# A decoder block on one core: the ConvFFN up projection as wide and narrow matmuls, and a gap between an adaLN row's copy and its transposes

## The chip, the cores and the metric

The kernel runs on one core of a Trainium2 chip, as one program in one launch. The metric is the device time in microseconds (us). Before the change the median of three runs is 1520.65 us (1518.46 to 1521.5). The engines named below are PE (TensorE, with PEld for its weight loads), DVE (VectorE), ACT (ScalarE), POOL (GpSimd) and SP (SyncE, whose queue issues nearly all the DMAs).

## The reference

One decoder block on 256 tokens of 2048 channels, all in float32. Two sub-layers, each wrapped in norms and in a shift, a scale and a gate that come from a conditioning vector c (adaLN):

```python
mod = (silu(c) @ w_ada + b_ada)                  # 6 rows of 2048: sh1, sc1, gt1, sh2, sc2, gt2
h = rms_norm(x, g_pre_mix) * (1 + sc1) + sh1
z = h @ w_in                                     # 2048 x 8000
mix = (g_a * mla(z) + g_b * swa(z)) @ w_o        # two attention mixers, gated
x = x + gt1 * rms_norm(mix, g_post_mix)
h = rms_norm(x, g_pre_ffn) * (1 + sc2) + sh2
u = causal_dwconv(h @ w_up, conv_w, conv_b)      # 2048 x 11264, then 3 taps along the tokens
y = (silu(u[:5632]) * u[5632:]) @ w_down         # 5632 x 2048
out = x + gt2 * rms_norm(y, g_post_ffn)
```

## The kernel before

**Precision.** Every large product is made of three float32r matmuls: a float32 operand is split into a high part (a cast on ACT, line 116 for weights and 151 for activations) and a low part (the difference, a subtraction on DVE, lines 117 and 152), and the product is hi*hi + hi*lo + lo*hi, accumulated in one PSUM bank. Lines 129 to 131 (`mm3`) do this with 128x128 weights held in the array and 256 token columns of activations streaming; lines 137 to 139 (`mm3t`) hold the activations and stream 512 columns of weights. The weights come as raw tiles of 512 KB (line 95), each split once and used once. Weight tiles rotate through pools: in the up projection 4 raw, 6 hi and 6 lo tiles.

**Stages.** Norm and first adaLN rows; the input projection; the attention stage; the output projection `down(w_o)`; the sandwich norm, which is a chain of small DVE and ACT steps (lines 672 to 688), then 32 transposes of the result back to channel-major on PE (line 143 for all transposes) and the modulated, split activations `h2` (lines 696, 697, 151, 152); the up projection, 44 steps j of two output blocks q (88 blocks); the down projection `down(w_down)`; the last norm and the stores.

**The up projection.** One block is 16 chunks of 128 input channels times three matmuls, all into the left half of a 512-column PSUM bank: 48 matmuls of 256 columns. A block's weights are two raw tiles; below, such a half block is called a *part* (24 matmuls). When a block is done, ACT makes `u` from the bank with the middle tap and the bias (line 738), and DVE adds the two other taps, reading the bank again (lines 739 and 740). Every second step ends in a SiLU on ACT (743), a product on POOL (746) and a split of the result. The first step's two blocks have their weights loaded during `down(w_o)`; the second step's weights are held back until a late point of the making of `h2`.

**The adaLN rows in the background.** `ada_gen` loads a row block of `w_ada` (512 KB), lets DVE multiply it by c and add it to an accumulator `acc` (lines 233 and 235), and yields; it does so 16 times, then sums `acc` over the partitions with 4 small matmuls (240) and copies the row to SBUF on ACT (242). `cols_gen` runs it for both halves of one row (32 yields) and then turns the row into columns with 4 small matmuls (290) and adds the bias (292). Three such rows (gt1, sc2, sh2, in this order in one list) run during the attention stage and `down(w_o)`, one (gt2) during the up projection. `pump` advances the list: it is called after each raw weight tile and takes a step as soon as `rate` has added up to 1 (rates 0.5, 0.8, 0.3 and 0.5 in four stages). `drain()` after `down(w_o)` runs whatever is left of the three rows.

**Order.** The Python code gives the program order; a list scheduler then places each engine's instructions, so neighbours in the code may be shifted. Each engine and each DMA queue works through its own list strictly as built.

## Time and profile before

| | |
|---|---|
| median of three runs | 1520.65 us |
| the profiled execution, its own time | 1520.17 us |
| its span in the trace | 1518.3 us |
| PE busy | 1472.3 us, 97% |
| PE weight loads busy | 1361.0 us, 90% |
| DVE busy | 1050.1 us, 69% |
| ACT busy | 754.4 us, 50% |
| POOL busy | 286.9 us, 19% |
| mean DMA rate | 235 GB/s |

Busy time is the union of an engine's instructions in the trace. A matmul is shown with a modelled end, so that neighbours overlap: what a stream of matmuls costs is read from the distance of their starts and not from their durations. The stages by time: input projection to about 300 us, attention to 650, `down(w_o)` to 745, the sandwich norm to 756, up projection from 756 to 1269, down projection to the end.

### The profile page before, as it was taken

Reading aid. Unit: us, or ns where it says so; the run is one execution under the profiler, and the core shown is the slowest. Engines: PE = TensorE matmul, PEld = TensorE weight load, DVE = VectorE, ACT = ScalarE, POOL = GpSimd, SP = SyncE. Lnnn points to the kernel's source line nnn. Section 1 sums busy time; section 2 is a strip of 40 time slices with the busy share of each in tenths; the row PEclk is TensorE's granted clock in tenths of the full one; section 3 lists DMA queues with packets and bytes.
Section 4 is the critical chain, followed back from the end, with each engine's and each line's share of the span. In section 5 each row is a group of like instructions: output and inputs, shape, how many; then the busy total and the mean of one; then the engine's idle time right before and its main releaser. Section 6 shows DMA issues by size and latency. Waiting matters only on the chain.

```text
span 1518.3 us, 27322 instructions
## 1 busy us (share of the span) xinstructions
PE 1472.3 (97%) x10914; PEld 1361.0 (90%) x10914; DVE 1050.1 (69%) x1384; ACT 754.4 (50%) x1165; POOL 286.9 (19%) x207
## 2 busy tenths in 40 slices
PE   7999999799999999999899999999999999999998
PEld 6988899789898898978799999999999999888886
DVE  3578868888787969777787777765666665444443
ACT  4534435545654655765564444554554454444342
POOL 0034215832525444320000010000000000000000
PEclk9999999999999999999999999999999999999999
DMA  9889868589587968669477788755556557666662
GB/s 371 295 313 328 308 234 262 178 264 306 175 306 240 298 197 274 197 208 358 183 250 259 254 277 266 225 181 183 182 181 190 182 181 242 191 193 192 194 193 99
DMA packets 101535, 357.14 MB, mean 235 GB/s; under 512 B 11760, under 2 KB 12208, under 8 KB 100896
## 3 DMA queue, kind: packets, MB, share of 16 engines
q1 hardware_dynamic: 99936, 350.82, 69.4%
q0 software_dynamic: 1472, 4.58, 1.2%
q8 instruction: 85, 1.39, 0.4%
q14 instruction: 42, 0.34, 0.1%
HBM read 351.11 MB, written 4.24 MB: 234 GB/s over the span
## 4 chain that ended last, share of the span: by engine, by line
PE 79%; DVE 9%; DMA 7%; issue 3%; ACT 1%; POOL 0%; DVEq 0%; SPq 0%; ACTq 0%; POOLq 0%
PE bk_mm L129 12%; PE bk_mm L131 12%; PE bk_mm L130 12%; PE bk_mm L137 4%; PE bk_mm L138 4%; PE bk_mm L139 4%; DMA raw<-in_w_ada_dram 4%; PE bk_sc L130 4%; PE bk_sc L129 4%; PE bk_sc L131 4%; PE bk_sc L138 3%; PE bk_sc L137 3%; PE bk_sc L139 3%; DVE wlo L117 3%; DVE acc L235 3%
## 5 line engine op out<-in xcount | busy, mean ns | idle before, releaser
L117 DVE TENSOR_TENSOR wlo<-raw,whi 128x1024 fp32r<-128x1024 f32 (+3 forms) x472 | 589.7, 1256 | 317.2 <-ACT whi L116 316.0
L116 ACT CAST whi<-raw 128x1024 fp32r<-128x1024 f32 (+3 forms) x472 | 478.1, 1019 | 531.7 <-PE bk_mm L130 161.6
L129 PE MATMUL bk_mm<-h_hi,whi 128*128 128x256 f32 x1824 | 522.6, 287 | 0.8 <-ACT h_hi L151 0.5
L131 PE MATMUL bk_mm<-h_hi,wlo 128*128 128x256 f32 x1824 | 518.0, 284 | 0.5 <-DVE wlo L117 0.5
L130 PE MATMUL bk_mm<-h_lo,whi 128*128 128x256 f32 x1824 | 518.4, 284 | 0.1
L129 PEld LDWEIGHTS bk_mm<-h_hi,whi 128*128 128x128 f32 x1824 | 350.9, 192 | 14.2 <-issue 8.7
L130 PEld LDWEIGHTS bk_mm<-h_lo,whi 128*128 128x128 f32 x1824 | 351.2, 193 | 1.1 <-issue 0.8
L131 PEld LDWEIGHTS bk_mm<-h_hi,wlo 128*128 128x128 f32 x1824 | 351.2, 193 | 1.2 <-DVE wlo L117 0.7
L235 DVE SCALAR_TENSOR_TENSOR acc<-raw,csil,acc 128x1024 f32<-128x1024 f32 (+1 forms) x141 | 188.6, 1337 | 58.2 <-DMA raw<-in_w_ada_dram 58.0
L129 PE MATMUL bk_sc<-h_hi,whi 128*128 128x256 f32 x560 | 158.7, 283 | 0.0
L130 PE MATMUL bk_sc<-h_lo,whi 128*128 128x256 f32 x560 | 158.6, 283 | 0.0
L131 PE MATMUL bk_sc<-h_hi,wlo 128*128 128x256 f32 x560 | 158.5, 283 | 0.0
L746 POOL TENSOR_TENSOR sa<-sa,u 128x512 f32<-128x512 f32 x22 | 32.7, 1486 | 469.1 <-DVE u L740 447.6
L129 PEld LDWEIGHTS bk_sc<-h_hi,whi 128*128 128x128 f32 x560 | 107.5, 192 | 0.4 <-ACT whi L116 0.4
L130 PEld LDWEIGHTS bk_sc<-h_lo,whi 128*128 128x128 f32 x560 | 107.5, 192 | 0.2 <-DVE h_lo L152 0.2
L131 PEld LDWEIGHTS bk_sc<-h_hi,wlo 128*128 128x128 f32 x560 | 107.5, 192 | 0.0
L363 POOL TENSOR_TENSOR pair<-pair,part 128x512 f32<-128x512 f32 x35 | 64.0, 1830 | 195.2 <-ACT part L362 195.1
L137 PE MATMUL bk_sc<-whi,g_hi 128*128 128x512 f32 x176 | 68.6, 390 | 0.0
L137 PE MATMUL bk_mm<-whi,g_hi 128*128 128x512 f32 x176 | 68.6, 390 | 0.0
L138 PE MATMUL bk_mm<-wlo,g_hi 128*128 128x512 f32 x176 | 68.5, 389 | 0.0
L139 PE MATMUL bk_mm<-whi,g_lo 128*128 128x512 f32 x176 | 68.5, 389 | 0.0
L138 PE MATMUL bk_sc<-wlo,g_hi 128*128 128x512 f32 x176 | 68.5, 389 | 0.0
(202 smaller groups left out, 2102.8 us busy)
## 6 DMA issues: line engine op xcount, KB each, us to landing
raw<-in_w_ada_dram SPq DMA_DIRECT2D x192, 512.0 KB, 5.0
raw<-in_w_up_dram SPq DMA_DIRECT2D x176, 512.0 KB, 4.3
raw<-in_w_in_dram SPq DMA_DIRECT2D x116, 512.0 KB, 5.1
raw<-in_w_down_dram SPq DMA_DIRECT2D x88, 512.0 KB, 4.4
raw<-in_w_o_dram SPq DMA_DIRECT2D x32, 512.0 KB, 5.0
raw<-in_w_uqn_dram SPq DMA_DIRECT2D x16, 384.0 KB, 4.1
bias<-trow POOLq DMA_DIRECT2D x16, 256.0 KB, 5.2
raw<-in_w_ukv_dram SPq DMA_DIRECT2D x16, 256.0 KB, 3.5
```

The source lines that it names most:

```text
L116: act.copy(hi[:, :n], raw[:, :n])
L117: dve.tensor_tensor(lo[:, :n], raw[:, :n], hi[:, :n].bitcast(F32), op=ALU.subtract)
L129: pe.matmul(o, wh, xh, start=start, stop=False)
L130: pe.matmul(o, wh, xl, start=False, stop=False)
L131: pe.matmul(o, wl, xh, start=False, stop=stop)
L137: pe.matmul(o, ch, wh, start=start, stop=False)
L138: pe.matmul(o, ch, wl, start=False, stop=False)
L139: pe.matmul(o, cl, wh, start=False, stop=stop)
L235: dve.scalar_tensor_tensor(acc[:, :w], r, csil[:, j:j + 1], acc[:, :w], op0=ALU.mult, op1=ALU.add)
L363: pool.tensor_tensor(pairs[i][:, :wd], pairs[i][:, :wd], part[:, :wd], op=ALU.add)
L746: pool.tensor_tensor(sa, sa, us[1], op=ALU.mult)
```

## The change

Three things.

1. In the up projection, `mm3w` takes two chunks at once. The activations' high and low part of a chunk now lie side by side in one tile, so one matmul of 512 columns computes hi*hi into the left half of the bank and hi*lo into the right half; then a matmul of 256 columns adds lo*hi to the left half. Two chunks go as wide, wide, narrow, narrow. At a block's end ACT copies the right half to a new SBUF tile `o`, DVE adds the left half to it, and the conv taps (ACT and DVE) read `o` instead of the bank.
2. For that, `split_pair` makes one tile of 1024 columns for two chunks instead of a hi and a lo tile, the pool `hp` has 8 such tiles instead of 16 of half the size, and the last stage's residual tiles are halves of these. The latent tiles of the attention stage keep the old form, written out in place.
3. In `cols_gen`, four bare yields stand between the second half's copy and the transposing matmuls. Each takes one step of `pump` without doing anything.

```diff
@@ -49,7 +49,7 @@
     const = ctx.enter_context(tc.tile_pool(name="const", bufs=1))
     dram = ctx.enter_context(tc.tile_pool(name="dram", bufs=1, space=bass.MemoryType.DRAM))
     hp_ctx = ExitStack()
-    hp = hp_ctx.enter_context(tc.tile_pool(name="hp", bufs=16, side="right"))
+    hp = hp_ctx.enter_context(tc.tile_pool(name="hp", bufs=8, side="right"))
     w_ctx = ExitStack()
     W = {"pool": w_ctx.enter_context(tc.tile_pool(name="wp1", bufs=1)), "n": NW1}
     psp = ctx.enter_context(tc.tile_pool(name="psp", bufs=1, space=PS))
@@ -125,14 +125,21 @@
 
     def mm3(o, w, x, start, stop):
 
-        (wh, wl), (xh, xl) = w, x
+        (wh, wl), (xh, xl, _) = w, x
         pe.matmul(o, wh, xh, start=start, stop=False)
         pe.matmul(o, wh, xl, start=False, stop=False)
         pe.matmul(o, wl, xh, start=False, stop=stop)
 
+    def mm3w(o, ws, xs, start, stop):
+
+        for i, (w, x) in enumerate(zip(ws, xs)):
+            pe.matmul(o, w[0], x[2], start=start and i == 0, stop=False)
+        for i, (w, x) in enumerate(zip(ws, xs)):
+            pe.matmul(o[:, :T], w[1], x[0], start=False, stop=stop and i == 1)
+
     def mm3t(o, w, x, half, start, stop):
 
-        (wh, wl), (xh, xl) = w, x
+        (wh, wl), (xh, xl, _) = w, x
         ch, cl = xh[:, half * P:half * P + P], xl[:, half * P:half * P + P]
         pe.matmul(o, ch, wh, start=start, stop=False)
         pe.matmul(o, ch, wl, start=False, stop=False)
@@ -146,12 +153,12 @@
 
     def split_pair(src, pl, tag, bufs, eng=dve):
 
-        hi = pl.tile([P, 512], F32R, tag=tag, bufs=bufs, name=tag + "_hi")
-        lo = pl.tile([P, 512], F32R, tag=tag, bufs=bufs, name=tag + "_lo")
-        i0 = act.copy(hi, src)
-        i1 = eng.tensor_tensor(lo, src, hi.bitcast(F32), op=ALU.subtract)
+        hl = pl.tile([P, 2, 2, T], F32R, tag=tag, bufs=bufs // 2, name=tag)
+        src = src.rearrange("p (j t) -> p j t", j=2)
+        i0 = act.copy(hl[:, :, 0], src)
+        i1 = eng.tensor_tensor(hl[:, :, 1], src, hl[:, :, 0].bitcast(F32), op=ALU.subtract)
         split_ins[:] = [i0, i1]
-        return [(hi[:, j * T:j * T + T], lo[:, j * T:j * T + T]) for j in range(2)]
+        return [(hl[:, j, 0], hl[:, j, 1], hl[:, j].rearrange("p a t -> p (a t)")) for j in range(2)]
 
 
     blk_ctx = ExitStack()
@@ -285,6 +292,9 @@
 
         for half in range(2):
             yield from ada_gen(a["w_ada2"][which][half], T, rows, half * T, None)
+
+        for _ in range(4):
+            yield
         ps = bank("tp")
         for b in range(4):
             pe.matmul(ps[:, 4 * b:4 * b + 4], rows[:, b * P:(b + 1) * P], ident[:, 0:P:32], start=True, stop=True)
@@ -404,7 +414,11 @@
             for j in range(2):
                 v = pr[:, j * T:j * T + T]
                 dve.scalar_tensor_tensor(v, v, gcol[:, gofs + 2 * i + j:gofs + 2 * i + j + 1], r, op0=ALU.mult, op1=ALU.mult)
-            res += split_pair(pr, blkp, "blk", NBLK, pool)
+            hi = blkp.tile([P, 512], F32R, tag="blk", name="blk_hi")
+            lo = blkp.tile([P, 512], F32R, tag="blk", name="blk_lo")
+            act.copy(hi, pr)
+            pool.tensor_tensor(lo, pr, hi.bitcast(F32), op=ALU.subtract)
+            res += [(hi[:, j * T:j * T + T], lo[:, j * T:j * T + T], None) for j in range(2)]
 
     def rope(x, n):
 
@@ -714,26 +728,28 @@
         e = j % 2
         if e == 0:
             us = [up.tile([P, 512], F32, tag=f"u{q}", name="u") for q in range(2)]
-        bs = [bank2()[:, :T] for q in range(2)]
+        bs = [bank2() for q in range(2)]
         if j == 0:
             wts = up0
-            for k in range(KC):
+            for k in range(0, KC, 2):
                 for q in range(2):
-                    mm3(bs[q], wts[q].cut(k * P), h2[k], k == 0, k == KC - 1)
+                    mm3w(bs[q], [wts[q].cut(i * P) for i in (k, k + 1)], h2[k:k + 2], k == 0, k == KC - 2)
             w_ctx.close()
             W.update(W2)
             ff = ctx.enter_context(tc.tile_pool(name="ff", bufs=1, reuse_waits="tile"))
         for q in range(2):
             fblk = q * NF + j
-            o = bs[q]
             if j:
                 with ExitStack() as order:
                     if j == 1:
                         order.enter_context(tc.issue_after(after_dve.ins))
                         order.enter_context(tc.issue_after(after_act.ins))
                     wt = Weights(a["w_up"][fblk], 2048)
-                for k in range(KC):
-                    mm3(o, wt.cut(k * P), h2[k], k == 0, k == KC - 1)
+                for k in range(0, KC, 2):
+                    mm3w(bs[q], [wt.cut(i * P) for i in (k, k + 1)], h2[k:k + 2], k == 0, k == KC - 2)
+            o = up.tile([P, T], F32, tag="o", name="o")
+            act.copy(o, bs[q][:, T:])
+            dve.tensor_tensor(o, o, bs[q][:, :T], op=ALU.add)
             u = us[q][:, e * T:e * T + T]
             act.activation(u, o, AF.Identity, scale=cw[:, 2, fblk:fblk + 1], bias=cw[:, 3, fblk:fblk + 1])
             dve.scalar_tensor_tensor(u[:, 1:], o[:, :T - 1], cw[:, 1, fblk:fblk + 1], u[:, 1:], op0=ALU.mult, op1=ALU.add)
@@ -749,8 +765,10 @@
     up_ctx.close()
 
     fin = ctx.enter_context(tc.tile_pool(name="fin", bufs=1, reuse_waits="tile"))
-    x2 = [[hp.tile([P, 512], F32, tag="h", name="x2") for g in range(4)] for t in range(2)]
-    y2 = [[hp.tile([P, 512], F32, tag="h", name="y2") for g in range(4)] for t in range(2)]
+    def halves(name):
+        b = [hp.tile([P, 1024], F32, tag="h", name=name) for _ in range(4)]
+        return [[b[2 * t + g // 2][:, g % 2 * 512:g % 2 * 512 + 512] for g in range(4)] for t in range(2)]
+    x2, y2 = halves("x2"), halves("y2")
     for t in range(2):
         for g in range(4):
             nc.sync.dma_start(x2[t][g], x1d[t * P:(t + 1) * P, g * 512:g * 512 + 512])
```

How the instructions move, at three places. The list that PE works through in the up projection, around the end of the gt2 row (`bk_tp<-acc,ones` is the sum over partitions, `bk_tp<-c_ident,rows` the transposing matmuls; `whi`, `wlo` are the weights' parts). Before:

```order
L129 MATMUL bk_sc<-h_hi,whi 128x256
L130 MATMUL bk_sc<-h_lo,whi 128x256
L131 MATMUL bk_sc<-h_hi,wlo 128x256
L240 MATMUL bk_tp<-acc,ones 32x256 x4
L290 MATMUL bk_tp<-c_ident,rows 128x4 x2
L129 MATMUL bk_mm<-h_hi,whi 128x256
...
L129 MATMUL bk_mm<-h_hi,whi 128x256
L130 MATMUL bk_mm<-h_lo,whi 128x256
L290 MATMUL bk_tp<-c_ident,rows 128x4 x2
L131 MATMUL bk_mm<-h_hi,wlo 128x256
```

After, at the same place:

```order
L136 MATMUL bk_sc<-h,whi 128x512 x2
L138 MATMUL bk_sc<-h,wlo 128x256 x2
L247 MATMUL bk_tp<-acc,ones 32x256 x4
L136 MATMUL bk_mm<-h,whi 128x512 x2
...
L136 MATMUL bk_mm<-h,whi 128x512 x2
L138 MATMUL bk_mm<-h,wlo 128x256 x2
L300 MATMUL bk_tp<-c_ident,rows 128x4 x4
L136 MATMUL bk_sc<-h,whi 128x512 x2
```

Two chunks now take four matmuls, two of 512 and two of 256 columns, where six of 256 stood. The four transposing matmuls, of which two stood right behind the sums and two 28 rows later, now stand together 65 rows behind the sums.

The list of the SP queue from the last loads of `down(w_o)` to the stores of the residual (`w_ada_1` is the sh2 row, `w_ada_3` the gt2 row, which the scheduler starts early; `w_up` the first up-projection weights). Before:

```order
L95 DMA raw<-in_w_ada_1_dram 128x1024 x2
L95 DMA raw<-in_w_up_dram 128x1024 x2
L95 DMA raw<-in_w_ada_3_dram 128x1024
L95 DMA raw<-in_w_up_dram 128x1024 x2
L95 DMA raw<-in_w_ada_1_dram 128x1024
L95 DMA raw<-in_w_up_dram 128x1024
L95 DMA raw<-in_w_ada_1_dram 128x1024 x3
L702 DMA x1d<-x_7860 128x2048 x2
L95 DMA raw<-in_w_up_dram 128x1024
```
After:

```order
L95 DMA raw<-in_w_ada_1_dram 128x1024 x2
L95 DMA raw<-in_w_ada_3_dram 128x1024
L95 DMA raw<-in_w_up_dram 128x1024 x4
L95 DMA raw<-in_w_ada_1_dram 128x1024
L95 DMA raw<-in_w_up_dram 128x1024
L95 DMA raw<-in_w_ada_1_dram 128x1024 x9
L716 DMA x1d<-x_7813 128x2048
L95 DMA raw<-in_w_ada_1_dram 128x1024 x2
L716 DMA x1d<-x_7813 128x2048
L95 DMA raw<-in_w_up_dram 128x1024
```

Behind the fourth of the last five `w_up` tiles there stand 4 more loads of the sh2 row before and 12 after, two of them behind the first store. The sh2 row's work has moved towards the end of `down(w_o)`, since the three rows take 12 more steps of `pump`.

The list of DVE from the sandwich norm of the second 128 tokens to the first chunk of `h2` (`acc` is a step of an adaLN row, `ss2s`, `r` the norm, `x` and `yg` the residual and the normed rows, `sh` the finished sh2 columns, `ht` the modulated activations). Before:

```order
L672 TENSOR_REDUCE ss_8578<-ssq 128x1
L654 TENSOR_TENSOR yg<-bk_mm,gate 128x512
L658 RECIPROCAL r_8581<-r_8581 128x1
L658 RECIPROCAL r_8577<-r_8577 128x1
L688 TENSOR_SCALAR yg<-x_7860,r_8581 128x512 x2
L678 SCALAR_TENSOR_TENSOR x_7860<-yg,r_8577,x_7860 128x512 x2
L292 TENSOR_TENSOR sh_148<-bk_tp,c_b_adaT 128x16
L678 SCALAR_TENSOR_TENSOR x_7860<-yg,r_8577,x_7860 128x512 x2
L681 TENSOR_REDUCE ss2s<-ss_8580 128x1
L658 RECIPROCAL r_8581<-r_8581 128x1
L688 TENSOR_SCALAR yg<-x_7860,r_8581 128x512 x2
L697 TENSOR_SCALAR ht<-bk_mm,s_147,sh_148 128x256 x2
```
After:

```order
L692 SCALAR_TENSOR_TENSOR x_7813<-yg,r_8561,x_7813 128x512 x4
L672 RECIPROCAL r_8565<-r_8565 128x1
L242 SCALAR_TENSOR_TENSOR acc<-raw,csil,acc 128x1024
L702 TENSOR_SCALAR yg<-x_7813,r_8565 128x512 x2
L695 TENSOR_REDUCE ss2s<-ss_8564 128x1
L242 SCALAR_TENSOR_TENSOR acc<-raw,csil,acc 128x1024
L672 RECIPROCAL r_8565<-r_8565 128x1
L242 SCALAR_TENSOR_TENSOR acc<-raw,csil,acc 128x1024
L702 TENSOR_SCALAR yg<-x_7813,r_8565 128x512 x2
L242 SCALAR_TENSOR_TENSOR acc<-raw,csil,acc 128x1024
L302 TENSOR_TENSOR sh_148<-bk_tp,c_b_adaT 128x16
L711 TENSOR_SCALAR ht<-bk_mm,s_147,sh_148 128x256 x2
```

Before, no step of `acc` is left here and `sh` is ready between two updates of `x`. After, four steps of `acc` stand among the last twelve rows, five more above them back to the first half's norm (where two stood), and `sh` comes last, directly ahead of `ht`.

## Rows read from the trace of the kernel before

**Rows 1.** The page: busy time of the engines, and the chain of waits that ended last, by engine.

```profile
PE 1472.3 (97%) x10914; PEld 1361.0 (90%) x10914; DVE 1050.1 (69%) x1384; ACT 754.4 (50%) x1165; POOL 286.9 (19%) x207
PE 79%; DVE 9%; DMA 7%; issue 3%; ACT 1%; POOL 0%; DVEq 0%; SPq 0%; ACTq 0%; POOLq 0%
```

**Rows 2.** Busy time by stretch: the up projection while the gt2 row runs beside it, and after that. Columns: stretch, its length, busy us (instructions) of PE, PEld, DVE, ACT, POOL, granted clock, DMA share, GB/s.

```profile
752.00:962.00 210.00, 207.33 (x1716) 205.35 (x1717) 164.74 (x196) 109.91 (x143) 15.17 (x9) 0.99 0.77 255
962.00:1264.00 302.00, 302.00 (x2519) 302.00 (x2518) 190.41 (x226) 148.28 (x183) 16.83 (x13) 1.00 0.59 186
```

**Rows 3.** Timeline of PE (start us, duration us), first and last of stretches of back-to-back matmuls: 48 matmuls of 256 columns in the up projection, then 15 matmuls of 512 columns in the down projection.

```profile
1050.54 0.28 PE L129 MATMUL bk_sc<-h_hi,whi 128*128 128x256 f32 x1
...
1056.30 0.28 PE L129 MATMUL bk_mm<-h_hi,whi 128*128 128x256 f32 x1
...
1272.17 0.39 PE L137 MATMUL bk_sc<-whi,g_hi 128*128 128x512 f32 x1
...
1275.57 0.39 PE L137 MATMUL bk_mm<-whi,g_hi 128*128 128x512 f32 x1
```

**Rows 4.** Timeline of DVE through the sandwich norm; in brackets the idle time before a row and what ended it.

```profile
737.94 0.16 DVE L672 TENSOR_REDUCE ss<-ssq 128x1 f32<-128x4 f32 x1 [2.82 <-ACT sqd L651]
...
738.61 1.27 DVE L235 SCALAR_TENSOR_TENSOR acc<-raw,csil,acc 128x1024 f32<-128x1024 f32 x1
...
739.92 1.28 DVE L235 SCALAR_TENSOR_TENSOR acc<-raw,csil,acc 128x1024 f32<-128x1024 f32 x1
741.12 2.73 DVE L678 SCALAR_TENSOR_TENSOR x<-yg,r,x 128x512 f32<-128x512 f32 x4
744.93 0.16 DVE L681 TENSOR_REDUCE ss2s<-ss 128x1 f32<-128x4 f32 x1 [1.07 <-ACT sq L680]
746.04 0.16 DVE L672 TENSOR_REDUCE ss<-ssq 128x1 f32<-128x4 f32 x1 [0.95 <-ACT sqd L651]
...
749.02 0.16 DVE L292 TENSOR_TENSOR sh<-bk_tp,c_b_adaT 128x16 f32<-128x16 f32 x1
...
752.27 0.88 DVE L688 TENSOR_SCALAR yg<-x,r 128x512 f32<-128x512 f32 x2
```

**Rows 5.** Timelines of PE, then ACT, in the same place: the sum, the transposing matmuls of the sh2 row, the transposes of the normed rows, the first up-projection matmul; the row's copy and the first modulated chunk on ACT.

```profile
745.21 0.64 PE L240 MATMUL bk_tp<-acc,ones 128*32 128x256 f32 x8
745.78 1.33 PE L290 MATMUL bk_tp<-c_ident,rows 128*128 128x4 f32 x8
...
752.81 3.68 PE L143 MATMUL bk_mm<-c_ident,yg 128*128 128x128 f32 x17 [4.81 <-DVE yg L688]
756.25 0.36 PE L129 MATMUL bk_sc<-h_hi,whi 128*128 128x256 f32 x1
...
746.09 0.36 ACT L242 COPY rows<-bk_tp 128x256 f32<-128x256 f32 x1
753.75 1.20 ACT L696 ACTIVATE ht<-bk_mm,sh,s 128x256 f32<-128x256 f32 x2
```

**Rows 6.** Who waited for whom (us in total, times, longest) from 780 to 960 us, then from 960 to 1260 us.

```profile
ACT whi L116 <- DMA raw<-in_w_up_dram: 48.5, 31, 3.7
DVE acc L235 <- DMA raw<-in_w_ada_dram: 29.6, 22, 2.8
ACT whi L116 <- PE bk_sc L130: 5.0, 3, 2.9
...
ACT whi L116 <- PE bk_mm L130: 83.4, 61, 2.4
ACT whi L116 <- PE bk_sc L130: 57.0, 42, 1.8
PE bk_tp L290 <- ACT rows L242: 1.9, 1, 1.9
```

**Rows 7.** Timelines of DVE and PE: the low parts of the weights of parts 17 and 66 (50 subtractions, the first and the last shown), and the starts of blocks 5 and 33 on PE (28 blocks apart, so parts 10 and 66).

```profile
798.32 1.22 DVE L117 TENSOR_TENSOR wlo<-raw,whi 128x1024 fp32r<-128x1024 f32 x1
...
944.81 1.21 DVE L117 TENSOR_TENSOR wlo<-raw,whi 128x1024 fp32r<-128x1024 f32 x1
...
786.83 0.28 PE L129 MATMUL bk_sc<-h_hi,whi 128*128 128x256 f32 x1
...
948.86 0.28 PE L129 MATMUL bk_sc<-h_hi,whi 128*128 128x256 f32 x1
```

**Rows 8.** Single lines (durations in ns: least, median, most): the copy of a 256-column PSUM row on ACT, and a two-operand step of DVE with a bank as an operand.

```profile
L242 ACT COPY rows<-bk_tp x8: 359/372/374, 331.2 to 960.5; 128x256 f32<-128x256 f32 x8
L739 DVE SCALAR_TENSOR_TENSOR u<-bk_mm,cw,u x53: 470/476/479, 781.7 to 1271.9; 128x255 f32<-128x255 f32 x53
```

**Rows 9.** Busy time by stretch, columns as in rows 2: three stretches of the attention stage, one while the sandwich norm begins, and two around the restart of PE after it.

```profile
500.00:550.00 50.00, 47.39 (x368) 44.09 (x367) 39.77 (x88) 34.16 (x90) 25.57 (x19) 1.00 0.81 266
550.00:600.00 50.00, 47.89 (x385) 45.47 (x384) 42.90 (x65) 26.07 (x56) 19.04 (x14) 1.00 0.74 245
600.00:650.00 50.00, 48.62 (x337) 43.40 (x337) 37.53 (x92) 33.98 (x82) 18.45 (x17) 0.97 0.61 193
...
735.00:740.00 5.00, 5.00 (x24) 4.14 (x23) 2.18 (x6) 0.98 (x3) 0.00 (x0) 1.00 0.01 4
...
753.00:756.00 3.00, 3.00 (x15) 2.64 (x14) 1.66 (x4) 2.76 (x5) 0.00 (x0) 0.52 0.28 112
756.00:759.00 3.00, 3.00 (x27) 2.76 (x25) 2.80 (x6) 2.54 (x6) 0.00 (x0) 1.00 0.00 0
```

## The prediction

> **What bounds the kernel now.** I read the page first: PE is busy for 97% of the span and makes up 79% of the chain that ended last, DVE 9% and DMA 7% [rows 1]. So time is won where PE's own work shrinks and nothing else is late behind it, and lost wherever PE is made to wait. Then the stretches of the up projection, the stage that the change rewrites: PE is busy 207.3 of 210 us while the gt2 row runs beside it, and all of 302 us after that, at full granted clock, with DVE at 78% and 63% [rows 2]. Next I wanted what a matmul costs, and took it from the distance of starts: 48 matmuls of 256 columns take 5.76 us, 120.0 ns each; 15 of 512 columns take 3.40 us, 226.7 ns each [rows 3]. The 256 columns between the two sizes cost 106.7 ns, so a matmul is 106.7 ns per 256 columns and 13.3 ns on top, whatever its width. Last, the waits: during the first stretch the casts of weights on ACT wait mostly for their loads (48.5 us in 31 waits), in the second for PE to free a tile (83.4 and 57.0 us) [rows 6]. The reader should see two regimes: with the adaLN loads the supply of weights is what runs short, without them PE is.
>
> **The wide matmuls.** The columns stay as they were: two chunks are 6 x 256 before and 2 x 512 + 2 x 256 after. What goes is two of six matmuls, so 16 of a block's 48, and with each of them 13.3 ns [rows 3]. A block falls from 5.76 to 5.55 us, by 0.213; all 88 blocks by 18.7 us.
>
> The Trainium skill speaks against this. TensorE: Matmul & The Clock Gate, section Back-to-back issue gap, gives a warm matmul as its columns over 2.4 GHz plus about 2.5 ns; by that rule the 1408 matmuls fewer are worth 3.5 us, an estimate from that page, and the change as a whole would cost time. The trace does not agree: its two pitches leave 13.3 ns at both widths [rows 3].
>
> **What of it arrives.** PE can gain only while weights are ahead of it. The low parts of parts 17 and 66 begin 146.49 us apart, 2.990 us per part; PE moves at 162.03 / 56 = 2.893 us per part [rows 7]. Part 17 was ready at 799.5 and, seven parts of 2.88 behind 786.83, used at 807.0: a lead of 7.5 us. Part 66 was ready at 946.0 and used at 948.9: 2.8 us. So already before, supply is slower than PE here, and PE lives on its lead. After, PE asks for a part every 2.77 us; the lead is gone after 7.5 / 0.22 = 34 parts, and from there PE runs at the pace of supply. With that pace unchanged, part 66 can come forward by its lead of 2.8 us and no more, instead of the 7.0 of 33 blocks.
>
> Will the pace hold? Each block gets a copy of 256 columns on ACT, as the row copy's 0.37 us, and an addition on DVE, nearest the tap's 0.48 us [rows 8]. Taps and bias then read `o` from SBUF, which I count as equal. In the stretch of 210 us ACT is busy 110 and DVE 165 [rows 2], and both wait for loads there, so their 33 x 0.37 = 12 and 33 x 0.48 = 16 us find room. But both queues work in order: ACT's bias step now waits for DVE's addition, which stands behind steps of `acc` that wait for their loads (29.6 us in 22 waits [rows 6]), and behind ACT's step stand the next casts. The bounds are wide: if all of 0.85 us per block went into the pace it would be 0.43 per part; if the casts' waits for PE (5.0 us in 3 waits [rows 6]) went because PE is quicker, the pace would gain 0.1. I take 0.04, a tenth of the upper bound, since loads end most of the waits: 50 x 0.04 = 2.0 us, which leaves 2.8 - 2.0 = **0.8 us** of the gain in this stretch. From part 66 on PE sets the pace [rows 2, 6], and the two additions are hidden (DVE 190 of 302 us busy): 55 blocks x 0.213 = **11.7 us**.
>
> **The four yields, where they help.** PE stood 1.9 us before the transposing matmuls of gt2, waiting for the row's copy, which was queued on ACT [rows 6]. With the transposes 65 rows later the copy is long done: **1.9 us** won. It is one wait in the whole span; the other three rows have none on PE to lose.
>
> **The four yields, where they cost.** Three rows now need 36 steps each instead of 32, so when `drain()` comes 12 steps are left over, and some 8 loads with their steps of `acc` move from the attention stage to the end of `down(w_o)`. In the new order nine steps of `acc` stand on DVE between the first norm and `ht`, where two stood. Before, the second half's norm begins at 746.04 and sh2 is ready at 749.0, well before `ht` at 753.75 [rows 4, 5]. After, I add DVE's list up from that same 746.04 (PE's end of `down(w_o)` sets it, and the one extra `acc` before it fits the idle 1.07 and 0.95 us there [rows 4]). A step of `acc` takes 1.20 from start to start, the four updates of x 2.7, each pair of yg 0.8, the gate product 0.6, the small steps together 0.6: six `acc` make 7.2, and all of it 12.6, so the last `acc` ends near 758.7. Then come the sum, the copy, the transposing matmuls and the bias, 1.9 us from the first sum to the last transpose in the old order [rows 5], with hops 2.6: `ht` starts near 761.3 instead of 753.75, **7.6 us** later, and PE has nothing else to do. Eight loads of 512 KB in a row need a free DMA: its share is 0.01 at 735 to 740 [rows 9], so I count no wait for them; if the six late steps each waited 1.35 us, as steps of `acc` did on average [rows 6], it would be 15.7. The lower end is 4, if the row's tail overlaps the norm. PE's clock falls to half in this pause now and is full again at 756 [rows 9]; the transposes run ahead of the first matmuls then as now, and at worst 3 us at half clock cost 1.5.
>
> **At nothing.** The joint hi and lo tiles hold the same bytes and are freed by the same stages; the last stage's halves wait for the stage before, long over when they are read. In the attention stage eight steps of `acc` are missing and some instructions change places. PE idles 6.1 of 150 us there [rows 9]: at best all of that goes; at worst as much again is added. I take 0.
>
> **Sum.** Against the profiled execution: 1520.17 - 0.8 - 11.7 - 1.9 + 7.6 = 1513.4 us. The median of the runs is 0.5 above that execution, so **1514 us**.
>
> **Rivals.**
> *The supply keeps up.* If the copy and the addition vanish in waits and casts no longer wait for PE, all 18.7 us arrive: 1520.65 - 18.7 - 1.9 + 7.6 = 1507.7 us. For it: the load waits of rows 6 are idle time. Against it: 2.99 us per part is slower than PE already. 18%.
> *The supply breaks: slower.* ACT's bias step waiting for DVE's addition, itself behind `acc`, holds the next cast, so each tile's load is issued later. The price is 64 parts times the pace lost. The gains of 2.8, 11.7 and 1.9 less the 7.6 leave 8.8 us, so it decides from 0.14 us per part on; at 0.22, half the upper bound, it is 14.1 us: 1525.9 us. For it: the loads already end most casts' waits; against it: ACT is only half busy. 10%.
> *The sh2 row is later still.* At the end of 15.7 us the sum is 8.1 us more: 1522. For it: five raw tiles serve twelve loads in a row; against it: a DMA with nothing else to do. 12%, most of it within 0.2%.
> *A matmul's 13.3 ns is not saved.* If the constant sits with something that the change leaves, as the page's smaller figure would have it, PE gains 3.5 us at the most, on both stretches: 1520.65 - 3.5 - 1.9 + 7.6 = 1522.9. Against it: both pitches. 5%.
>
> **Numbers.** The forecast has 55%. A measurement of this kernel can tell about 0.2% from no change, so faster means under 1517.6 and slower over 1523.7. The forecast's own range is 1508 to 1519, by the bounds of the pace, the pause and the attention stage. Faster: nearly all of the forecast and the first rival, with a small part of the late row, 0.74. Same: the rest of the forecast, most of the late row and of the unsaved constant, 0.16. Slower: 0.10. The range of 8 in 10 takes in half of the first rival and the edge of the late row: 1505 to 1520.
>
> **What would show it.** In the trace after: wide matmuls 226.7 ns and narrow ones 120 ns apart, in a block of 5.55 us from 970 us on (else the 13.3 ns is wrong); gaps on PE in the second half of the gt2 stretch, behind `whi` or `wlo` (no gaps: the first rival; gaps from its beginning: the second); a pause on PE between `down(w_o)` and the first up-projection matmul near 18.6 us instead of 11, ended by sh2; no wait at the transposing matmuls of gt2. The forecast is wrong if that pause stays as it was, or if the gt2 stretch is longer than 210 us plus the pause.

## The result, and the profile after

The changed kernel takes **1529.24 us** (median of 8 runs, 1522.83 to 1531.02), the kernel before, beside it on the same chip, 1520.16 (8 runs): ratio **1.0056**, 95% interval 1.0041 to 1.0070. Forecast were 1514 us and a range of 1505 to 1520. The change costs 9 us where 6 were to be won, and the time lies outside the range.

The profiled execution took 1522.83 us (span 1521.1), the fastest of the eight; a second profile of the same instructions in the same order, below, took 1527.41 (span 1525.6). Three marks on the timelines of PE and ACT divide the loss:

| us | before | after | after, again |
|---|---|---|---|
| last matmul of `down(w_o)` starts | 744.9 | 754.7 | 755.3 |
| first `ht` starts (ACT) | 753.8 | 771.0 | 772.3 |
| last up-projection matmul starts | 1269.3 | 1271.7 | 1276.3 |
| first `ht` to last up matmul | 515.5 | 500.7 | 504.0 |

So 10 us are lost before `down(w_o)` ends, 7.4 to 8.1 more before `ht`, and the up projection gives 14.8 back in the one execution, 11.5 in the other. The last two were forecast; the first 10 us were not.

**The pause.** PE's waits from 735 to 800 us, then DVE's rows from the second half's sum to the last late step of `acc` and to the finished sh2 columns:

```profile
PE bk_mm L150 <- DVE yg L702: 8.4, 1, 8.4
PE bk_mm L150 <- ACT yg L700: 1.6, 1, 1.6
PE bk_mm L150 <- DVE ht L711: 1.5, 1, 1.5
```

```profile
755.87 0.16 DVE L686 TENSOR_REDUCE ss<-ssq 128x1 f32<-128x4 f32 x1 [0.98 <-ACT sqd L665]
...
767.13 1.28 DVE L242 SCALAR_TENSOR_TENSOR acc<-raw,csil,acc 128x1024 f32<-128x1024 f32 x1
770.76 0.18 DVE L302 TENSOR_TENSOR sh<-bk_tp,c_b_adaT 128x16 f32<-128x16 f32 x1 [2.36 <-PE bk_tp L300]
```

These answer to [rows 4, 5]. From the second half's sum to the end of the last late `acc` DVE needs 767.13 + 1.28 - 755.87 = 12.5 us; sh2 is ready 2.4 us later, and `ht` starts at 771.0.

**The up projection.** One block of 32 matmuls on PE's timeline, from the first wide pair of one block to that of the next (a row holds two back-to-back matmuls):

```profile
1054.49 0.63 PE L136 MATMUL bk_mm<-h,whi 128*128 128x512 f32 x2
1054.96 0.39 PE L138 MATMUL bk_mm<-h,wlo 128*128 128x256 f32 x2
1055.19 0.62 PE L136 MATMUL bk_mm<-h,whi 128*128 128x512 f32 x2
...
1060.06 0.63 PE L136 MATMUL bk_sc<-h,whi 128*128 128x512 f32 x2
```

A block takes 1060.06 - 1054.49 = 5.57 us, against 5.76 before [rows 3]. The waits at gt2's transposes are gone, and those that are left from 800 to 1000 us are for low parts of weights: 1.5 us in the first execution (first fence), 3.6 in the second:

```profile
PE bk_mm L138 <- DVE wlo L117: 1.0, 1, 1.0
PE bk_sc L138 <- DVE wlo L117: 0.5, 2, 0.3
```

```profile
PE bk_mm L138 <- DVE wlo L117: 1.8, 4, 0.9
PE bk_sc L138 <- DVE wlo L117: 1.8, 2, 1.5
```

**The attention stage.** PE's row of the stretches of [rows 9]; columns: stretch, length, busy us (instructions), granted clock, DMA share, GB/s:

```profile
500.00:550.00 50.00, 45.12 (x325) 0.93 0.60 193
550.00:600.00 50.00, 48.03 (x389) 1.00 0.83 272
600.00:650.00 50.00, 48.22 (x356) 0.97 0.68 226
```

The first stretch has lost 2.3 us of PE, a granted clock of 0.93 where it was 1.00, and a quarter of its traffic (193 GB/s for 266). Of the clock by itself little can be read: the kernel with the yields of sh2 and gt2 alone, below, shows 0.93 in this stretch too. Cut finer, in the same columns:

```profile
500.00:510.00 10.00, 10.00 (x80) 1.00 0.39 107
510.00:520.00 10.00, 10.00 (x75) 1.00 0.02 5
520.00:530.00 10.00, 5.12 (x29) 0.86 0.80 236
530.00:540.00 10.00, 10.00 (x72) 0.80 0.87 304
```

From 510 to 520 us the memory is nearly silent; ten us later PE stands still for half of the time and then runs below its full clock (0.86, 0.80). The queue of SP shows why. First its waits from 480 to 530 us, then its timeline:

```profile
SPq L95 <- DVE wlo L117: 17.5, 8, 5.1
SPq L95 <- DVE acc L240: 11.8, 1, 11.8
```

```profile
506.53 0.33 SPq L95 DMA_DIRECT2D raw<-in_w_ada_dram  x1
518.78 0.33 SPq L95 DMA_DIRECT2D raw<-in_w_ukv_dram  x1
```

For 12 us no load is issued: the next, weights of the attention, waits 11.8 us for a raw tile that the first `acc` step of s2's second half still holds. That step stands on DVE behind an attention output (`tm`) and the score masks, which wait for PE, and waits 0.96 us itself for PE's sums of the half before:

```profile
512.49 0.69 DVE L587 SCALAR_TENSOR_TENSOR tm<-pair,bk_o 128x512 f32<-128x512 f32 x1 [5.04 <-PE bk_o L585]
515.60 0.35 DVE L549 CUSTOM_DVE_ANT_0 sm<-bk_sc,c_cmask,c_sink 128x128 f32<-128x128 f32 x1 [2.42 <-PE bk_sc L541]
...
518.00 0.75 DVE L240 TENSOR_SCALAR acc<-raw,csil 128x1024 f32<-128x1024 f32 x1 [0.96 <-PE bk_tp L247]
```

And this is what it does to PE, further on in its timeline:

```profile
525.48 0.39 PE L144 MATMUL bk_mm<-whi,blk_hi 128*128 128x256 f32 x1 [1.40 <-ACT whi L116]
529.04 0.58 PE L145 MATMUL bk_mm<-wlo,blk_hi 128*128 128x256 f32 x1 [2.64 <-DVE wlo L117]
```

That is not the whole loss of the stage. From 320 to 745 us PE's waits add up to 21.2 us, 8.2 more than before; 5.1 of them are for weights (the two lines below), where before there were none. The other 3.1 us are longer waits for the attention's own steps on DVE and POOL.

```profile
PE bk_mm L145 <- DVE wlo L117: 3.7, 2, 2.6
PE bk_mm L144 <- ACT whi L116: 1.4, 1, 1.4
```

A step of background work that DVE reaches late holds a tile, the tile holds the in-order load queue, and the loads behind are not its own but those that PE needs next.

### The profile page after: what moved, and what is told of

The parts are those of the page before. It is cut to its first block, busy times and chain, and to the rows that moved or that the text cites. A ratio compares the mean times of both kernels' runs of the same rounds, so it can differ in the third digit from the quotient of the medians.

```text
span 1521.1 us, 24741 instructions
## 1 busy us (share of the span) xinstructions
PE 1459.5 (96%) x9506; PEld 1282.4 (84%) x9506; DVE 1078.2 (71%) x1472; ACT 782.0 (51%) x1253; POOL 287.8 (19%) x207
## 4 chain that ended last, share of the span: by engine, by line
PE 57%; DMA 11%; DVE 9%; issue 2%; ACT 2%; POOL 2%; DVEq 0%; ACTq 0%; POOLq 0%
PE bk_mm L136 8%; DMA raw<-in_w_ada_dram 7%; PE bk_sc L136 5%; PE bk_mm L138 4%; PE bk_mm L145 4%; PE bk_mm L146 4%; PE bk_mm L144 4%; DVE wlo L117 4%; PE bk_sc L144 3%; PE bk_sc L145 3%; PE bk_sc L146 3%; PE bk_mm L131 3%; PE bk_mm L129 3%; PE bk_mm L130 3%; PE bk_sc L138 3%
## 5 line engine op out<-in xcount | busy, mean ns | idle before, releaser
L129 PE MATMUL bk_mm<-h,whi 128*128 128x256 f32 x976 | 282.5, 290 | 1.6 <-DVE pair L375 1.6
L131 PE MATMUL bk_mm<-h,wlo 128*128 128x256 f32 x976 | 277.2, 285 | 0.4 <-DVE wlo L117 0.4
L130 PE MATMUL bk_mm<-h,whi 128*128 128x256 f32 x976 | 277.1, 284 | 0.0
L136 PE MATMUL bk_mm<-h,whi 128*128 128x512 f32 x848 | 266.4, 395 | 0.0
L129 PEld LDWEIGHTS bk_mm<-h,whi 128*128 128x128 f32 x976 | 187.2, 192 | 15.5 <-issue 9.3
L138 PEld LDWEIGHTS bk_mm<-h,wlo 128*128 128x128 f32 x848 | 158.9, 188 | 39.5 <-DVE wlo L117 2.3
L131 PEld LDWEIGHTS bk_mm<-h,wlo 128*128 128x128 f32 x976 | 187.0, 192 | 1.5 <-issue 0.8
L130 PEld LDWEIGHTS bk_mm<-h,whi 128*128 128x128 f32 x976 | 187.4, 192 | 0.6 <-issue 0.6
L136 PE MATMUL bk_sc<-h,whi 128*128 128x512 f32 x560 | 177.2, 398 | 0.0
L138 PE MATMUL bk_mm<-h,wlo 128*128 128x256 f32 x848 | 167.0, 278 | 1.0 <-DVE wlo L117 1.0
L136 PEld LDWEIGHTS bk_mm<-h,whi 128*128 128x128 f32 x848 | 129.1, 189 | 0.4 <-ACT o L751 0.4
L138 PEld LDWEIGHTS bk_sc<-h,wlo 128*128 128x128 f32 x560 | 105.6, 189 | 26.2 <-DVE wlo L117 1.3
L762 POOL TENSOR_TENSOR sa<-sa,u 128x512 f32<-128x512 f32 x22 | 33.4, 1520 | 465.3 <-DVE u L756 415.4
L138 PE MATMUL bk_sc<-h,wlo 128*128 128x256 f32 x560 | 110.9, 279 | 0.5 <-DVE wlo L117 0.5
L136 PEld LDWEIGHTS bk_sc<-h,whi 128*128 128x128 f32 x560 | 85.7, 190 | 0.8 <-issue 0.4
L144 PE MATMUL bk_sc<-whi,g 128*128 128x512 f32 x176 | 68.6, 390 | 0.0
```

What stands on the lines that cost most here:

```text
L129: pe.matmul(o, wh, xh, start=start, stop=False)
L130: pe.matmul(o, wh, xl, start=False, stop=False)
L131: pe.matmul(o, wl, xh, start=False, stop=stop)
L136: pe.matmul(o, w[0], x[2], start=start and i == 0, stop=False)
L138: pe.matmul(o[:, :T], w[1], x[0], start=False, stop=stop and i == 1)
L144: pe.matmul(o, ch, wh, start=start, stop=False)
```

## The experiments

All times stand beside runs of the kernel before on the same chip; their medians were 1519.9 to 1520.8 us. The marks are those of the table above, from each profiled execution: end of `down(w_o)`, first `ht`, and from there to the last up-projection matmul. The column gt1 is one mark more: ACT's copy of the second half of the gt1 row, ahead of every empty step (414.3 in the kernel before, 414.6 in the changed one).

| kernel | us | ratio (95%) | gt1 | w_o | ht | up |
|---|---|---|---|---|---|---|
| tiles only | 1519.3 | 0.9994 (0.9980 to 1.0009) | 414.9 | 744.2 | 753.8 | 513.7 |
| before + all yields | 1537.9 | 1.0119 (1.0097 to 1.0141) | 414.5 | 753.9 | 771.1 | 514.7 |
| before + gt2's yields | 1518.9 | 0.9993 (0.9981 to 1.0004) | 417.3 | 746.3 | 755.2 | 513.8 |
| before, half rate | 1519.3 | 0.9993 (0.9982 to 1.0004) | 416.7 | 748.1 | 756.9 | 514.1 |
| wide, no yields | 1514.5 | 0.9957 (0.9941 to 0.9973) | 414.5 | 743.4 | 753.0 | 511.5 |
| wide, gt2's yields | 1506.2 | 0.9904 (0.9885 to 0.9923) | 415.9 | 744.1 | 753.7 | 501.5 |
| the same with sh2's | 1509.3 | 0.9929 (0.9909 to 0.9950) | 415.8 | 747.6 | 757.1 | 506.1 |
| wide, gt1's and gt2's | 1525.0 | 1.0038 (1.0023 to 1.0053) | 413.0 | 755.9 | 769.0 | 502.7 |
| wide, s2's and gt2's | 1516.8 | 0.9981 (0.9966 to 0.9996) | 411.6 | 746.2 | 759.3 | 504.3 |
| wide, gt1 six, gt2 four | 1530.0 | 1.0064 (1.0049 to 1.0078) | 412.7 | 759.1 | 776.0 | 502.5 |
| after, again | 1528.3 | 1.0053 (1.0040 to 1.0066) | 414.8 | 755.3 | 772.3 | 504.0 |
| after, faster pump | 1514.7 | 0.9962 (0.9946 to 0.9977) | 382.8 | 752.5 | 760.6 | 504.3 |
| transposes later, no empty steps | 1507.7 | 0.9913 (0.9896 to 0.9931) | 414.2 | 744.2 | 753.8 | 503.3 |
| wide, gt2's yields, half rate | 1501.3 | 0.9873 (0.9859 to 0.9888) | 413.7 | 740.9 | 750.5 | 497.8 |
| wide, no yields, half rate | 1506.5 | 0.9906 (0.9890 to 0.9922) | 415.7 | 744.7 | 754.3 | 497.6 |
| transposes later, half rate | 1501.2 | 0.9870 (0.9851 to 0.9888) | 415.1 | 745.6 | 755.2 | 497.2 |
| after, short `acc` | 1508.6 | 0.9923 (0.9907 to 0.9939) | 409.0 | 738.1 | 750.6 | 507.8 |
| wide, gt2's yields, short `acc` | 1492.7 | 0.9813 (0.9798 to 0.9828) | 409.9 | 727.1 | 735.2 | 506.4 |

### Which part costs, which gains

The theory (A): the yields cost all that is lost. Rivals: the joint tiles do (B); copy and addition break the supply (C).

```diff
-        for _ in range(4):
-            yield
```


> The changed kernel without the four yields: wide matmuls, joint tiles, copy and addition stay. Theory A (the four yields cost everything that was lost ahead of the up projection: 9.9 us by the end of the w_o stage and 7.4 us more in the pause behind it; the up projection itself gained 14.9 us, 1.9 of it by the yields): 1520.2 - 13.0 = 1507 us, w_o ending at the same time as in the kernel before, pause 11 us. Theory B (the joint hi and lo tiles, not the yields, cost the 9.9 us): 1517 us, w_o 9.9 us late, pause 11 us. Theory C (copy and addition break the supply in most runs, which the profiled run of the changed kernel missed): over 1513 us, with gaps on PE in the first 210 us of the up projection.

The kernel before with these two lines added:

> The kernel before with the four yields alone: narrow matmuls, separate hi and lo tiles. Theory A: 1520.2 + 9.9 + 7.4 - 1.9 = 1535.6 us, w_o ending 10 us later and the pause 18.4 us. Theory B: 1520.2 + 7.4 - 1.9 = 1525.7 us, w_o ending as before. Theory C says nothing else than A here.

```diff
-        for _ in range(4):
+        for _ in range(4 if dst is gt2 else 0):
```


> The changed kernel with the four yields for the gt2 row alone. Theory A: 1.9 us faster than without yields, so 1505 us, with no wait at the transposing matmuls of gt2. Theory B: 1515 us. Theory C: over 1511 us. If instead the wait at these transposes was no loss (supply sets the pace there anyway): the same time as without yields.

The fourth undoes yields, wide matmuls, copy and addition and keeps the tiles.

> The changed kernel without yields and without wide matmuls, copy and addition: only the joint hi and lo tiles and the last stage's joint halves are left. Theory A: as before, 1520 us within 2 us. Theory B: 1530 us. Theory C: 1520 us.

1514.5, 1537.9, 1506.2 and 1519.3 us. B falls (tiles alone: no difference), and so does C with the third kernel (1506.2 us, where C asked for over 1511). A stands: the yields alone put `down(w_o)` 9.0 us and `ht` 17.3 us back, as in the changed kernel. The best of the four has the yields for gt2 alone. One thing missed: without any yields I expected 1507, and it is 1514.5. In that profile the wait at gt2's transposes is not 1.9 us [rows 6] but 4.94, and PE's granted clock is 0.50 right after it:

```profile
964.17 1.01 PE L297 MATMUL bk_tp<-c_ident,rows 128*128 128x4 f32 x4 [4.94 <-ACT rows L249]
```

```profile
960.00:965.00 5.00, 0.83 (x4) 0.85 0.48 172
965.00:970.00 5.00, 5.00 (x17) 0.50 0.59 201
```

ACT shows what the row's copy was queued behind: a cast that waited 2.75 us for POOL, two casts of weights, a bias step and the block's own copy, new with the change. How much of the longer wait is due to that copy (0.36 us) isn't separated.

```profile
960.58 0.62 ACT L158 CAST g<-sa 128x512 fp32r<-128x512 f32 x1 [2.75 <-POOL sa L759]
961.10 1.04 ACT L116 CAST whi<-raw 128x1024 fp32r<-128x1024 f32 x1
962.05 0.60 ACT L751 ACTIVATE u<-o,cw 128x256 f32<-128x256 f32 x1
962.55 1.03 ACT L116 CAST whi<-raw 128x1024 fp32r<-128x1024 f32 x1
963.49 0.36 ACT L748 COPY o<-bk_sc 128x256 f32<-128x256 f32 x1
963.75 0.37 ACT L249 COPY rows<-bk_tp 128x256 f32<-128x256 f32 x1
```

### Which row's yields

The condition in the same line names gt1, s2 or sh2 beside gt2; the fourth kernel keeps all yields and changes the rates:

> The changed kernel with the yields for gt1 and gt2, not for s2 and sh2. Theory A (the empty steps push adaLN loads behind: the order of loads and acc steps in the attention stage and the late sh2 row cost the 23 us between 1506 and 1529; gt1's and s2's yields share it): six acc steps stand between the first norm and the first ht instead of two or nine, so about 4 us of the pause's 7.4, and some 5 of the 9.9 us ahead of it: 1515 us. Theory D (one bad place decides: the load queue on SP that stands 12 us still near 507 to 519 us, behind an acc step that is late on DVE; it is there only where s2's yields are): 1506 + 4 = 1510 us, no such stop of the queue.

> The changed kernel with the yields for s2 and gt2. Theory A: six acc steps between the first norm and ht, 4 us of the pause, and some 5 us ahead of it: 1515 us. Theory D: the 12 us stop of SP's queue is there and costs most of the 9.9 us: 1506 + 4 + 8 = 1518 us.

> The changed kernel with the yields for sh2 and gt2. The four empty steps come after sh2's last load, so no load and no acc step moves, and the drain passes them at once. Theories A and D: as with gt2's yields alone, 1506 us within 2 us. If the transposes of a row cost by standing late in themselves: up to 1510.

```diff
-RATES = (0.5, 0.8, 0.3, 0.5)
+RATES = (0.5625, 0.9, 0.3375, 0.5)
```


> The changed kernel with all its yields, and the three rates ahead of the up projection raised by 36/32 (0.5625, 0.9, 0.3375), so that the rows are done as early as with 32 steps: no acc step is left between the first norm and ht. Theory A: the pause is 11 us again and the attention stage loses little: 1506 to 1510 us. Theory D: the pause is 11 us, the attention stage loses up to 10 us if SP's queue stops at such a place: 1506 to 1516. If the empty steps cost by something else than the lateness of loads: 1520 or more.

Against some 1507 us, gt1's yields cost 18, s2's 10; together they cost 22, so the costs don't add. A had expected 1515 us with gt1's and 1506 to 1510 with the faster pump, and they are 1525.0 and 1514.7: its amounts don't hold. The kernel with sh2's has every engine's instructions in the same order as that with gt2's alone, so 1509.3 against 1506.2 (and 3.5 us at the end of `down(w_o)`) is what two runs of one kernel differ by; smaller differences are not read below. D was wrong about the row: the 12 us stop of SP is there with gt1's yields (504.5 us), not with s2's. The pause, by late `acc` steps, came as expected with s2's: 759.3 - 746.2 = 13.1 us from the end of `down(w_o)` to `ht`, 3.5 more than with gt2's yields alone. With the faster pump the pause is as short as before (8.1 us), yet `down(w_o)` ends 8.4 us late, with no 12 us stop of SP: to be done in time is not enough.

The mark at the end of `down(w_o)` also carries what two runs differ by before any empty step. The way from the mark gt1 to it is freer of that. In the eleven kernels with full `acc` steps and no empty steps of gt1 and s2 it takes 327.3 to 331.7 us; with s2's 334.6, with all yields at the old rates 339.4 to 340.5, with gt1's 342.9. So s2's yields cost some 5 us there (3 over the longest of the eleven), not the 2 that the marks w_o seem to show. They show the loss in another form: from 320 to 745 us PE never waits for weights, but steps of `acc` wait on DVE for their own loads, and the attention's steps stand behind them. From 555 to 640 us these waits come to 13.1 us (first line); with gt2's yields alone, at the same place of the list (559 to 644 us), to 3.0 (second).

```profile
DVE acc L242 <- DMA raw<-in_w_ada_dram: 13.1, 11, 4.2
```

```profile
DVE acc L242 <- DMA raw<-in_w_ada_dram: 3.0, 3, 1.4
```

The longest of these waits, on the timelines of DVE and then PE: `tm`, an attention output, comes behind the late step on DVE, and PE waits 1.99 us for it.

```profile
608.12 1.28 DVE L242 SCALAR_TENSOR_TENSOR acc<-raw,csil,acc 128x1024 f32<-128x1024 f32 x1 [4.22 <-DMA raw<-in_w_ada_dram]
609.32 0.68 DVE L587 SCALAR_TENSOR_TENSOR tm<-pair,bk_o 128x512 f32<-128x512 f32 x1
610.05 0.94 PE L584 MATMUL bk_o<-pT,vt 128*128 128x256 f32 x2 [1.99 <-DVE tm L587]
```

### Is it that one stop?

```diff
-        for _ in range(4):
+        for _ in range({id(gt1): 6, id(gt2): 4}.get(id(dst), 0)):
```


> The changed kernel with six yields for gt1 (four before), four for gt2, none for s2 and sh2. Theory D2 (what costs in the attention stage is one stop of SP's queue of 12 us near 505 us, behind the first acc step of s2's second half, which stands on DVE behind the score masks; in the order with four yields it stands there, with six it stands behind a wlo instead): no such stop, the w_o stage ends no later than with the gt2 row's yields alone plus 3 us, eight acc steps between the first norm and ht, so a pause some 5 us longer: 1507 + 3 + 5 = 1515 us. Theory A (each empty step costs in proportion; four of gt1 cost 18 us): 1507 + 27 = 1534 us.

1530.0 us, `down(w_o)` 15 us late (346.5 us behind the mark gt1). The 12 us stop is gone, as the order had told; but SP now has gaps between loads of 6 to 8 us near 511, 589, 597 and 605 us (with gt2's yields alone the first of 6 us and more comes at 626 us), and PE's waits for weights come to 6.1 us from 320 to 745 us, where the kernel with gt2's yields alone has none. D2 falls: the stop is the form that the loss takes in one order, not its cause. A's amount (27 us) is near: 23.

The rest of the question is what in the shifted steps does it, DVE's time or the loads. All yields, and gt2's alone, with cut steps:

```diff
-  dve.scalar_tensor_tensor(acc[:, :w], r, csil[:, j:j + 1], acc[:, :w], op0=ALU.mult, op1=ALU.add)
+  c = w if on_pe else P
+  dve.scalar_tensor_tensor(acc[:, :c], r[:, :c], csil[:, j:j + 1], acc[:, :c], op0=ALU.mult, op1=ALU.add)
```


> The changed kernel, all yields, with the steps of acc of the four rows cut to 128 of 1024 columns (the adaLN rows are then not computed in the rest), so that a step takes some 0.2 us of DVE instead of 1.28; the loads stay in the changed kernel's order. To be read beside the same cut with gt2's yields alone. Theory F1 (yields cost ahead of the up projection because acc steps of 1.28 us then stand on DVE in front of what PE waits for): the end of the w_o stage is within 3 us of that of its partner, instead of 10 us later. Theory F2 (they cost because loads of weights on SP wait for raw slots that a late acc step holds, or are issued in a worse order): still 7 us or more later than the partner.

> The partner: yields for gt2 alone, the same cut of acc. F1 and F2: faster than the 1507 us of the full steps, since DVE is freed by some 126 x 1.08 us of which little is on the path: 1498 to 1506 us. The difference to the partner with all yields is what counts: under F1 the pause's few us alone, under F2 10 us and more.

1508.6 and 1492.7 us, the second 5 us under its range. Both are faster than with full steps (a cut one takes 0.35 us), but the yields' cost stays: `down(w_o)` ends at 738.1 and 727.1 us, 11.0 apart, and `ht` starts 15.4 apart. SP again stops for the first step of `acc`, with all yields (first fence, 480 to 515 us), and not with gt2's alone (second, 320 to 620 us):

```profile
SPq L95 <- DVE acc L240: 12.4, 1, 12.4
```

```profile
SPq L95 <- DVE acc L240: 6.2, 4, 3.1
```

So F1 falls: ahead of the end of `down(w_o)` it is not the time that the steps take on DVE that costs, but when they come. F2 is what is left, and the stop of SP is seen; but how the held-back loads reach PE is not followed step by step. From 320 us to the end of `down(w_o)` PE waits 12.0 us with all yields and 5.1 with gt2's alone, and only 1.6 of the 12.0 are for weights, the rest for the attention's steps on the other engines. Nor do short steps rule out the form seen with s2's yields, steps that wait for their own loads. (The cut steps also let the scheduler place other instructions differently; SP's list stayed that of the partner with full steps in both, but for one or two loads near the end of `down(w_o)`.)

```diff
-            yield from ada_gen(a["w_ada2"][which][half], T, rows, half * T, None)
+            for n, _ in enumerate(ada_gen(a["w_ada2"][which][half], T, rows, half * T, None)):
+                yield
+                if half == 0 and n == 3 and pend:
+                    pend.pop()()
+        if dst is gt1 or dst is s2:
+            pend.append(lambda: turn_row(dst, bofs, gofs))
+            return
...
```

(`turn_row` holds the transposes and the bias that followed here, `pend` starts as an empty list, and gt2 keeps its four yields.)

> The changed kernel with the transposes of gt1 and s2 still four steps after their row's copy, but these steps are the first four loads of the next row, so no step is empty; gt2 keeps its four yields. SP's and POOL's lists are those of the kernel with gt2's yields alone. Theory A (the empty steps cost, since loads and acc steps shift): 1507 us within 3. Theory G (it is the place of the transposes themselves on PE, or of the row's bias on DVE, that costs): 1515 us or more.

1507.7 us, all marks as with gt2's yields alone. G falls. Late transposes of gt1 and s2 cost nothing; empty steps do.

### The supply in the gt2 stretch

> The changed kernel without sh2's yields only. Those come after sh2's last load, in the drain, and move nothing, so every engine has the instructions of the changed kernel in its order. This is the changed kernel a second time: 1529 us. The question is where its usual run loses the 6 us that the profiled one (1522.8) did not. Theory E (supply in the gt2 stretch): idle of PE from 850 to 1000 us of 5 us and more, against 1.5 in the profiled run. Rival: the 6 us lie ahead of the up projection, with its first matmul at 779 us instead of 773.5.

1528.3 us. The profiled run is 4.6 us above the first profile: 0.6 at the end of `down(w_o)`, 0.7 in the pause, 3.3 in the up projection. E holds for most of it, though PE's idle time from 850 to 1000 us was 3.7 us, not 5.

> The kernel before with yields for the gt2 row alone. With wide matmuls these yields were worth 1514.5 - 1507 = 7 us. If the wait for the row's copy is worth its 1.9 us of idle here, as the prediction took it: 1518 us. If it is worth 7 us in every version: 1513. If supply sets the pace there anyway: 1520, no difference.

1518.9 us, within what can be told of both 1518 and 1520; 1513 is excluded. With narrow matmuls these yields are worth about 1 us, by the interval 3 at most; with wide ones 5 to 8.

```diff
-RATES = (0.5, 0.8, 0.3, 0.5)
+RATES = (0.5, 0.8, 0.3, 0.25)
```


> The changed kernel with yields for gt2 alone and the adaLN rate of the up projection halved (0.25 instead of 0.5: one load per four parts), so that gt2's 32 loads lie under 128 parts instead of 64. Theory E (the loads of gt2 make the supply of weights slower than PE, and what the wide matmuls save there is lost): PE has no idle time between 800 and 1250 us, all 88 blocks take 5.57 us or less, and the time falls from 1507 to 1501 to 1503 us, with less spread. Rival: the copy and the addition set the pace, not the loads: the idle time stays, spread over the longer stretch, 1507 us or more.

> The kernel before with the adaLN rate of the up projection halved (0.25), nothing else. With wide matmuls this was worth 6 us. Theory E (narrow matmuls leave PE slower than supply, or so nearly that the lead lasts): no idle time to win but gt2's 1.9 us, so 1518 to 1520.5 us. If the half rate is worth 6 us here too, E is wrong in that the shortage was there before the change: 1514 us.

1501.3 us with wide matmuls, 1519.3 with narrow ones. E holds: the shortage belongs to the faster PE. (Of the 7.0 us between its profile and that of its partner at the full rate 3.8 lie in the up projection. The others lie nearly all ahead of the end of `down(w_o)`, where the marks are no further apart than those of two runs of one kernel.) From 800 to 962 us PE is busy 160.50 of 162 us in the changed kernel (first line), all of it at half rate (second); columns as in [rows 2]:

```profile
800.00:962.00 162.00, 160.50 (x919) 138.16 (x919) 135.21 (x176) 87.53 (x127) 12.37 (x7) 1.00 0.80 266
```

```profile
800.00:962.00 162.00, 162.00 (x936) 140.91 (x935) 122.43 (x164) 89.13 (x131) 14.81 (x7) 1.00 0.69 231
```

And ACT's casts there wait 56.3 us for their loads in the changed kernel (first line), 17.8 at half rate (second):

```profile
ACT whi L116 <- DMA raw<-in_w_up_dram: 56.3, 33, 3.9
```

```profile
ACT whi L116 <- DMA raw<-in_w_up_dram: 17.8, 15, 2.9
```

Idle time tells only part of it. The starts of blocks 5 and 33 on PE, as in [rows 7], in the changed kernel (first fence) and at half rate (second):

```profile
804.13 0.63 PE L136 MATMUL bk_sc<-h,whi 128*128 128x512 f32 x2
...
963.66 0.62 PE L136 MATMUL bk_sc<-h,whi 128*128 128x512 f32 x2
```

```profile
783.36 0.63 PE L136 MATMUL bk_sc<-h,whi 128*128 128x512 f32 x2
...
939.41 0.63 PE L136 MATMUL bk_sc<-h,whi 128*128 128x512 f32 x2
```

The 28 blocks took 162.03 us with narrow matmuls. With wide ones they take 159.53 us, in the second execution 162.73 (805.51 to 968.24), and at half rate 156.05, which is 28 times 5.57. At the full rate the wide matmuls bring nearly nothing here.

Two more, at half rate, with no yields at all and with the transposes moved:

> Wide matmuls with gt2's half rate and no yields at all. At the full rate gt2's yields were worth 7 us (1514.5 against 1507), of which the trace without them shows one wait of 4.9 us for the row's copy and a clock of 0.84 behind it. If that wait is a matter of ACT's backlog in the crowded stretch: it is short here, 1501 to 1503 us, and the yields are worth nothing any more. If it comes from the copy's place in ACT's list alone (behind the block's own copy, which waits for PE): still 4 us and more, 1506 to 1509 us.

> Wide matmuls with gt2's half rate and yields, and gt1's and s2's transposes moved behind the first four loads of the next row without empty steps. If nothing but the empty steps and the supply mattered: the same as half rate with gt2's yields alone, 1501 us within 3.

Without yields: 1506.5 us (4 runs, 1502.9 to 1507.5); with moved transposes: 1501.2. The second is as expected. The first is inconclusive: its profiled run, the fastest, has no wait at gt2's transposes, which speaks for the crowded stretch, but the other runs are 4 us slower and were not seen in a profile. The fastest version found is thus the wide matmuls with yields for gt2 alone and half its rate: 1501.3 us, 1.3% under the kernel before, 1.8% under the changed one.

## Why the prediction was wrong

By its own steps:

- **13.3 ns per matmul saved: right, a little large.** A block falls to 5.57 us, not 5.55: 0.19 of the 0.213 us. The rival "not saved" falls. Two pitches alone could not have told that the 13.3 ns are the same at both widths, since any two fit such a sum; the new block is the test. The Trainium skill (TensorE: Matmul & The Clock Gate, section Back-to-back issue gap) gives about 2.5 ns on top of the columns, and gives it for a single isolated matmul, a limit that the prediction does not mention. Taken over to this stream it would leave a block at 5.72 us, an estimate from that page; the trace, with 5.57, does not agree.
- **Supply keeps only part of the gain in the gt2 stretch: right.** By 515.5 - 500.7 the up projection gained 14.8 us in the first execution and 11.5 in the second; the three terms added up to 0.8 + 11.7 + 1.9 = 14.4. Up to the start of block 33, where 0.8 us were forecast, it gained 2.4 in the first and lost 0.9 in the second (195.1 us behind the first `ht` before, 192.7 and 196.0 after); from there on it gained 12.4 in both, where 11.7 + 1.9 = 13.6 were forecast. That the lead works as a buffer, so that PE loses in one run what late loads ate of it, would fit both and was not tested. Halving the loads of gt2 brings up the gain to 515.5 - 497.8 = 17.7.
- **Copy and addition: right.** 0.36 and 0.41 us (0.37 and 0.48 taken). Not foreseen: without yields the wait for gt2's row copy grows from 1.9 us to 4.9, with a clock of 0.50 behind it; the new copy stands in front of the row copy on ACT, but so do casts of weights and one that waited 2.75 us for POOL. The yields' worth there was mis-sized, 1.9 for 5 to 8, once matmuls are wide.
- **The late sh2 row: right.** DVE's list from the second half's norm to the last `acc` was added up to 12.6 us and took 12.5; PE's pause was put at 18.6 us and was 18.8 from the last matmul of `down(w_o)` (754.7) to the first of the up projection (773.5), 19.8 in the second execution.
- **"At nothing: in the attention stage eight steps of acc are missing and some instructions change places. I take 0", with bounds of 6.1 us either way: this is the step that failed.** It measured +9.8 and +10.4 us, outside its bounds, and that is the forecast's error: 6 us won become, with these 10 and the 3 to 4 us of the usual run's supply, the 9 us lost (1514 + 10 + 3 = 1527, near the second profiled execution's 1527.41 and 2 us under the median). Two faults lie in it. The step counted what left the stage (work) and not what moved (eight loads and their `acc` steps, in an in-order queue that also carries the weights). And its bound was PE's idle time before, doubled; late loads and late steps make waits that were not there, 8.2 us more from 320 to 745 us, 5.1 of them for weights.

That the 10 us ahead of the end of `down(w_o)` are caused by the empty steps of gt1 and s2, and not by the place of the transposes, the tiles or the time of the steps on DVE, is shown by the runs. Why one order loses 5 us and another 17 is seen only in the orders traced here, in two forms: loads that SP holds back, and steps that wait for their own loads in front of the attention's. No rule for it was found, what each form costs was not separated, and a version that keeps the empty steps but frees SP's queue was not tried.
